# A second level of seven-product multiplication for product 6 of the gate and up stage of a two-layer encoder

## Chip, cores and metric

The kernel runs on one core of a Trainium2 chip. The metric is the device time of one execution in microseconds (us); less is better. Before the change it is 2160.32 us, the median of 3 runs (2157.54 to 2161.28).

## What is computed

Two encoder layers work on 1024 tokens of width 1024: a token mixer with memory heads, an output projection, and then a dense SwiGLU channel mixer with an inner width of 2816. The change lies in the first half of that mixer, the product `h @ w_gate_up[i]`:

```python
    for i in range(DEPTH):                                   # DEPTH = 2
        ...
        x = x + jnp.concatenate([y_tok, y_mem], axis=-1) @ w_out[i]
        h = rmsnorm(x, norm_ffn[i])
        gu = h @ w_gate_up[i]                                # (1024, 1024) @ (1024, 5632)
        x = x + (jax.nn.silu(gu[..., :D_FF]) * gu[..., D_FF:]) @ w_down[i]
    return rmsnorm(x, norm_final)
```

## The kernel before

**Precision.** Every float32 operand is kept as a rounded part and a rest (`hi`, line 105, a cast on ScalarE, ACT; `lo`, line 108, a subtraction on VectorE, DVE). A product of two operands is three matmuls (`three`, line 125): rounded by rounded, rounded by rest, rest by rounded. The weight is the operand that is loaded into the array (LDWEIGHTS, "PEld" in the profile), the activations stream past it, 512 columns at a time.

**Units and products.** The 2816 inner columns are 22 units of 128 (`Pair`, line 823). One unit holds 128 gate columns and 128 up columns; with the 1024 tokens in two halves and the 1024 rows of contraction in two halves this is a 2 by 2 by 2 block product, done in seven products instead of eight (0 to 6). Each of the seven has a contraction of 512 in four steps of 128, so it is 4 x 3 = 12 matmuls on 512 columns. The left sides are gate and up halves of the weight and their sums and differences: GpSimd (POOL) makes these in the tile `wS` (`prepare`, line 830). The right sides `B[0]` to `B[6]` are made once for each layer from the normalized activations (`right_sides`, line 965, for 1 to 6).

**Weight buffers.** `prepare` is called for every second product; it takes one tile `wgu` (tag `whl`, three buffers) that holds the left sides of two products, rounded parts and rests. Product 6 has a tile to itself. A unit so takes four tiles for its seven products. Two raw tiles for each unit are loaded by SyncE (SP) ahead of use (`load_gu`, line 926; five raw buffers).

**Sums and reads.** Products 0, 2, 4 and 6 of a unit use the PSUM bank `X`, products 1, 3 and 5 a bank `Y`. Products 2 and 4 are added in place to what `X` holds, and 5 to what 3 left in `Y`. So `read` (line 884) copies `X` after product 0 (`g1`), after 2 (`g2`) and after 4 (`c1`), and `Y` after 3 (`c2`), each copy on ACT and before the next product goes to that bank. Product 6 overwrites `X`, and DVE takes it from `c1` and multiplies by the activated gate `g1`. After every second unit `hand_over` (line 1001) writes right sides for the next stage to memory.

**Order.** `order` (lines 917 to 920) lists the products by hand: the first four units are interleaved, from the fifth on each unit runs 0 to 6. `gate_up` (line 1025) goes through it with `lead = 4`: before each product it prepares the one four places later. The recording layer puts instructions of one engine in another order than this where it expects one to be ready sooner, so the order on an engine is read from the built program. Each engine works its own list off in that order. While the last unit runs, the down projection (`left_side`, `right_side`, lines 1057 and 1100) is prepared.

Of the kernel before, what the change touches and what calls it, by code (L numbers as in the profile page):

```python
# [9 lines left out]
F32 = mybir.dt.float32  # L10
# [31 lines left out]
def trunk_kernel(ctx: ExitStack, tc: tile.TileContext, a: dict, out: bass.AP):  # L42
# [323 lines left out]
    for layer in range(2):  # L366
# [425 lines left out]


        with tc.tile_pool(name=f"fp{layer}", bufs=1, reuse_waits="tile") as fp:
            phase[:] = fp, 21, 5
            wide[:] = True, 2

            def pair(src, dst):
# [17 lines left out]
            norms = [Norm(), Norm()]  # L816

            B = [[None] * 4 for _ in range(7)]
            def load_x(m, f):
                x[m][f] = temp("x")  # L820
                nc.sync.dma_start(x[m][f], (a["x"] if is_a else x_d)[m][:, f * HS : (f + 1) * HS])

            class Pair:
# [6 lines left out]
                def prepare(self, n):  # L830

                    n -= n % 2
                    if n in self.left:
                        return
                    g1, g2 = self.raw[0][:, :HS], self.raw[0][:, HS:]
                    if n > 0:
                        u1, u2 = self.raw[1][:, :HS], self.raw[1][:, HS:]
                    sub = lambda o, p_, q_: nc.gpsimd.tensor_tensor(o, p_, q_, op=ALU.subtract)  # L838
                    s = self.raw[0]
                    if n == 2:  # L840
                        self.s = fp.tile([P, D], F32, tag="S", name="wS", bufs=2)
# [42 lines left out]
                def read(self, n):  # L884
                    self.seen.add(n)
                    X, Y = self.X, getattr(self, "Y", None)
                    add = lambda o, p_, q_, op=ALU.add: nc.vector.tensor_tensor(o, p_, q_, op=op)
                    if n == 0:
                        self.g1 = temp("g1")
                        nc.scalar.copy(self.g1, X)  # L890
                    elif n == 1:
                        add(self.g1, Y, self.g1)
                        nc.scalar.activation(self.g1, self.g1, AF.Silu)
                    elif n == 2:
                        self.g2 = temp("g2")
                        nc.scalar.copy(self.g2, X)
                    elif n == 3:
                        self.c2 = temp("c2")
                        nc.scalar.copy(self.c2, Y)  # L899
                    elif n == 4:  # L900
                        self.c1 = temp("c1")
                        nc.scalar.copy(self.c1, X)
                        add(self.c2, self.c2, self.c1)
                        if 5 in self.seen:
                            add(self.c2, self.c2, self.g2, ALU.mult)
                    elif n == 5:
                        add(self.g2, Y, self.g2)
                        nc.scalar.activation(self.g2, self.g2, AF.Silu)
                        if 4 in self.seen:
                            add(self.c2, self.c2, self.g2, ALU.mult)  # L910
                    else:
                        add(self.c1, self.c1, X, ALU.subtract)
                        add(self.c1, self.c1, self.g1, ALU.mult)

            us = [Pair(j) for j in range(NF)]
# [49 lines left out]
            def right_sides():  # L965
# [28 lines left out]
                for k in range(4):  # L994
                    B[6][k] = pair(x[k + 4][0], h_op(k))
                    yield

            def keep(i, p, t):
                nc.sync.dma_start(b_d[layer][i][:, p * HS : (p + 1) * HS], t)

# [24 lines left out]
            def gate_up():  # L1025
                run_some(rest, 1)
                load_gu()
                for i, (u, n) in enumerate(order):
                    if i + lead < len(order):
                        v, n_ = order[i + lead]  # L1030
                        v.prepare(n_)
                    u.product(n)
                    u.read(n)
                    run_some(rest, 1 if i < 2 * first else 2)
                    if n == 6 and u.j % 2:
                        hand_over(u.j // 2, us[u.j - 1], u)
                    yield u, n


            wd = a["w_dn"][layer].rearrange("(p i) r c -> p i r c", i=2)  # L1040
# [73 lines left out]
            def residual(i):  # L1114

                if i in (0, 2, 3, 4):
                    m0, f = {0: (0, 1), 2: (0, 0), 3: (4, 0), 4: (4, 1)}[i]
                    for m in range(m0, m0 + 4, 2):
                        t = fp.tile([P, 2, HS], F32, tag="S", name="xr", bufs=2)
# [83 lines left out]
            for u, n in gate_up():  # L1203
                if u.j == NF - 1 and n in (2, 3, 4):
                    keep_rows(n - 2)
                    if n > 2:
                        left_side(0, n - 3)
                if u.j == NF - 1 and n in (3, 4, 5):
                    right_side(0, n - 3)
# [127 lines left out]
```

## Time and profile before

| | |
|---|---|
| profiled execution, its own time | 2156.92 us |
| its span in the trace | 2155.1 us |
| mean granted TensorE clock | 0.993 |
| gate and up, busy of DVE / ACT / POOL in 1590 to 1670 us | 42.91 / 29.20 / 23.88 of 80 us |
| HBM read and written | 210.40 MB and 68.94 MB, 130 GB/s over the span |
| `b_d` stores of the stage | 154, of 256 KB |
| `wgu_raw` loads of the stage | 92 issues |

The rows of the profile name a line of the kernel, an engine, an operation and the tiles (out, arrow, in). In grouped rows the last number before the bar is the mean time of one instruction in ns, and after the bar stands the idle time of the engine before these instructions and who ended it. In rows of the timeline the first number is the start in us from the begin of the span, the second the length, "x12" the number of instructions merged, and the brackets hold the idle time before it and who ended that. A matmul's end is modelled, so matmuls overlap in the rows; their pace is read from starts.

### The profile page before, as it was taken

The page shows a single profiled execution, that of the slowest core. Times are in us where ns is not written, and L with a number is a line of the kernel's source. Part 1 is how long each engine was busy: PE and PEld are TensorE (multiplying, and loading weights), DVE is VectorE, ACT ScalarE, POOL GpSimd, SP SyncE. Part 2 cuts the span into 40 slices and gives each one's busy share as a digit, 9 for nine tenths or more (in the row PEclk, how much of TensorE's full clock was granted, in tenths as well). Part 3 has the DMA queues.
Part 4 walks back from the last instruction along what each step waited for, and adds up shares of the span by engine and source line. Part 5 has one row for each costly group of instructions (what it writes and reads, how often), then busy time and mean ns, then how long its engine had stood idle before and what let it go on. Part 6 is the DMA issues. An engine that isn't in the chain of part 4 may idle for free.

```text
span 2155.1 us, 28039 instructions
## 1 busy us (share of the span) xinstructions
PE 2113.1 (98%) x9946; PEld 1740.9 (81%) x9946; DVE 1417.9 (66%) x2314; ACT 1045.6 (49%) x1988; POOL 498.2 (23%) x545
## 2 busy tenths in 40 slices
PE   7999999999999999999999999999999999999997
PEld 6788888788888888888778888887888888888886
DVE  7677787776555555867776666677855564568675
ACT  6577785443333334344466566653533333344442
POOL 0344330223232320000233223203223323210000
PEclk9999999999999999999999999999999999999998
DMA  6321018323223236856232222274233222277662
GB/s 247 101 94 49 31 60 299 111 90 131 88 93 113 98 119 223 315 204 210 90 101 65 71 65 81 70 263 148 74 103 117 98 100 101 98 237 262 203 217 92
DMA packets 120076, 287.22 MB, mean 133 GB/s; under 512 B 12288, under 2 KB 18688, under 8 KB 119936
## 3 DMA queue, kind: packets, MB, share of 16 engines
q1 hardware_dynamic: 112896, 272.57, 37.8%
q10 hardware_dynamic: 7040, 12.85, 1.6%
q8 instruction: 79, 1.29, 0.2%
q14 instruction: 61, 0.50, 0.1%
HBM read 210.40 MB, written 68.94 MB: 130 GB/s over the span
## 4 chain that ended last, share of the span: by engine, by line
PE 43%; issue 4%; DVE 2%; ACT 2%; POOL 1%; DMA 0%; DVEq 0%; SPq 0%; POOLq 0%; ACTq 0%
PE X L879 11%; PE mm L139 9%; PE Y L879 8%; PE X L1171 5%; PE Y L1171 4%; PE po L139 2%; PE S L559 2%; PE O L622 1%; PE pT L602 1%; ACT p L574 0%; DMA b_raw<-b_d 0%; PE bc L242 0%; DVE pl L109 0%; DVE wqk L109 0%; PE vtr L419 0%
## 5 line engine op out<-in xcount | busy, mean ns | idle before, releaser
L879 PE MATMUL X<-hT,wgu 128*128 128x512 f32 x1056 | 259.1, 395 | 0.0
L879 PE MATMUL Y<-hB,wgu 128*128 128x512 f32 x1056 | 256.8, 392 | 1.6 <-ACT c L899 1.6
L879 PE MATMUL X<-hB,wgu 128*128 128x512 f32 x1056 | 247.8, 390 | 0.0
L1171 PE MATMUL X<-hB,wd 128*128 128x512 f32 x1056 | 242.1, 390 | 0.0
L879 PEld LDWEIGHTS X<-hT,wgu 128*128 128x128 f32 x1056 | 198.2, 188 | 47.3
L879 PEld LDWEIGHTS Y<-hB,wgu 128*128 128x128 f32 x1056 | 198.5, 188 | 46.3 <-ACT c L899 2.5
L879 PEld LDWEIGHTS X<-hB,wgu 128*128 128x128 f32 x1056 | 198.3, 188 | 41.7
L1171 PEld LDWEIGHTS X<-hB,wd 128*128 128x128 f32 x1056 | 198.1, 188 | 41.9 <-issue 1.0
L106 ACT CAST wgu<-wS 128x1024 fp32r<-128x1024 f32 x88 | 92.4, 1051 | 259.9 <-POOL wS L838 157.0
L587 POOL TENSOR_SCALAR p<-p,stat 128x384 f32<-128x384 f32 (+1 forms) x256 | 141.0, 569 | 312.1 <-DVE stat L584 212.2
L109 DVE TENSOR_TENSOR wgu<-wgu_raw,wgu 128x1024 fp32r<-128x1024 f32 (+1 forms) x88 | 84.7, 963 | 189.8 <-ACT wgu L106 189.8
L139 PE MATMUL mm<-hT,wqk 128*128 128x512 f32 x672 | 199.8, 405 | 0.1
L139 PE MATMUL po<-yT,wo 128*128 128x512 f32 x768 | 184.7, 394 | 0.0
L1171 PE MATMUL Y<-hB,wd 128*128 128x512 f32 x792 | 180.2, 389 | 0.0
L1171 PEld LDWEIGHTS Y<-hB,wd 128*128 128x128 f32 x792 | 148.7, 188 | 30.8
L139 PEld LDWEIGHTS po<-yT,wo 128*128 128x128 f32 x768 | 142.5, 188 | 29.5 <-issue 1.0
L838 POOL TENSOR_TENSOR wS<-wgu_raw 128x512 f32<-128x512 f32 x44 | 73.5, 1671 | 378.6 <-DVE wgu L109 378.6
L109 DVE TENSOR_TENSOR wgu<-wS,wgu 128x1024 fp32r<-128x1024 f32 x88 | 109.7, 1247 | 62.6 <-ACT wgu L106 62.6
L233 POOL TENSOR_TENSOR nr<-nv,neg_half 128x4 f32<-128x4 f32 (+1 forms) x11 | 11.7, 1063 | 587.0 <-DVE nv L232 586.8
L106 ACT CAST hB<-b_raw 128x512 fp32r<-128x512 f32 x154 | 88.8, 618 | 116.0 <-DMA b_raw<-b_d 106.4
L574 ACT ACTIVATE p<-p,stat 128x256 f32<-128x256 f32 (+1 forms) x192 | 112.3, 586 | 52.0 <-DVE stat L570 49.5
L106 ACT CAST wgu<-wgu_raw 128x1024 fp32r<-128x1024 f32 (+1 forms) x88 | 73.4, 835 | 122.5 <-PE Y L879 73.7
(161 smaller groups left out, 3913.3 us busy)
## 6 DMA issues: line engine op xcount, KB each, us to landing
wgu_raw<-in_w_gu SPq DMA_DIRECT2D x92, 512.0 KB
wd_raw<-in_w_dn SPq DMA_DIRECT2D x70, 512.0 KB
b_raw<-b_d SPq DMA_DIRECT2D x70, 512.0 KB
b_d<-c SPq DMA_DIRECT2D x88, 256.0 KB
b_d<-t SPq DMA_DIRECT2D x66, 256.0 KB
wo_raw<-in_w_out SPq DMA_DIRECT2D x32, 512.0 KB
x<-in_x SPq DMA_DIRECT2D x32, 256.0 KB
xr_d<-x ACTq DMA_DIRECT2D x32, 256.0 KB
```

The costliest lines, as they stand in the source:

```text
L106: nc.scalar.copy(dst, src)
L109: (eng or nc.vector).tensor_tensor(dst, src, h.bitcast(F32), op=ALU.subtract)
L139: nc.tensor.matmul(ps[:, :n], l, r, start=start and i == 0 and j == 0, stop=stop and i == len(order) - 1 and j == 2,)
L233: nc.gpsimd.tensor_tensor(r[:, :nb], v[:, :nb], neg_half[:, :nb], op=ALU.pow)
L559: nc.tensor.matmul(s_[:, :n], Q[self.h][:, qb * P : (qb + 1) * P], k, start=j == 0, stop=j == 1)
L574: nc.scalar.activation(p[:, :n], p[:, :n], AF.Exp, bias=m1, scale=-1.0, accum_out=s1)
L587: nc.gpsimd.tensor_scalar(p[:, :n], p[:, :n], ri[:, i : i + 1], 1.0, op0=ALU.mult, op1=ALU.mult)
L602: nc.tensor.transpose(tr[:, j * P : (j + 1) * P], p[:, j * P : (j + 1) * P], ident)
L622: nc.tensor.matmul(o[:, c0 : c0 + w * P], self.value(j), t[:, s0 : s0 + w].rearrange("p j q -> p (j q)"), start=j == js[0] and t is self.p ...
L838: sub = lambda o, p_, q_: nc.gpsimd.tensor_tensor(o, p_, q_, op=ALU.subtract)
L879: nc.tensor.matmul(ps, l, r, start=n in (0, 1, 3, 6) and k == 0 and i == 0, stop=k == 3 and i == 2, skip_group_check=True,)
L1171: nc.tensor.matmul(bank, l, r, start=i in (0, 1, 3, 6) and p == 0 and n == 0, stop=p == HF - 1 and n == 2, skip_group_check=True,)
```

## The change

From the fifth unit on two units a and b are taken together. Their products 6 have one right side, `B[6]`, so together they are a block product of 256 rows by a contraction of 512 by 512 columns. It is split in two in each direction and made by seven products (class `Fourth`), each of 128 rows by a contraction of 256 (two steps) by 256 columns: 7 x 2 x 3 = 42 matmuls on 256 columns, in place of 2 x 12 = 24 on 512. There are nine such pairs in each of the two layers.

- **Left sides.** `Fourth.prepare` casts the raw `u2` halves of both units into one tile `wgu` (called w4 below: a11, a12, a21, a22) and four combinations, which POOL makes with five 128x256 operations in a tile `wS4`, into another `wgu` tile (called ws4: s1 to s4). A pair takes 3 + 3 + 2 = 8 tiles, as before, from the same three buffers.
- **Right sides.** Four combinations of the blocks of `B[6]` are made once for each layer at the end of `right_sides` (eight 128x256 subtractions, four casts and four rests of 128x512; tiles `q4` and `q4h`).
- **Order.** Unit a runs 0 to 5, unit b runs 0, 1, 2, 4, then piece A, product 3 of b, piece B, product 5 of b, piece C. A is a11 and a12 (12 matmuls), B is s2 and s1 (12), C is s3, s4 and a22 (18). A, B and C use one bank of `Y`'s pool and the bank `O`.
- **Reads.** DVE subtracts the pieces from `c1` of a and b. Since b runs 4 before 3, the sum of `c2` and `c1` moves to whichever comes later.
- The pools change to 26 buffers for 128x512 tiles (from 21) and three for `wS` (from two); the kernel asks for 1024 bytes of scratch for DMA descriptors. At the end of the stage the down projection's first loads are hung on the new order's last places.

```diff
-            phase[:] = fp, 21, 5
+            phase[:] = fp, 26, 5
...
                     elif n == 3:
                         self.c2 = temp("c2")
                         nc.scalar.copy(self.c2, Y)
+                        if 4 in self.seen:
+                            add(self.c2, self.c2, self.c1)
                     elif n == 4:
                         self.c1 = temp("c1")
                         nc.scalar.copy(self.c1, X)
-                        add(self.c2, self.c2, self.c1)
+                        if 3 in self.seen:
+                            add(self.c2, self.c2, self.c1)
...
+            class Fourth:
+                def prepare(self, n):
+                    if self.w is not None:
+                        return
+                    r, h = [u.raw[1][:, HS:] for u in self.units], HS // 2
+                    s = fp.tile([P, D], F32, tag="S", name="wS4", bufs=3)
+                    s1, s2, s3, s4 = (s[:, i * h : (i + 1) * h] for i in range(4))
+                    sub = lambda o, p_, q_: nc.gpsimd.tensor_tensor(o, p_, q_, op=ALU.subtract)
+                    nc.gpsimd.tensor_tensor(s1, r[1][:, :h], r[1][:, h:], op=ALU.add)
+                    sub(s3, r[0][:, :h], r[1][:, :h])
+                    sub(s2, s1, r[0][:, :h])
+                    sub(s4, r[0][:, h:], s2)
+                    w = wp.tile([P, 2, D], F32R, tag="whl", name="wgu", bufs=3)
+                    for i in range(2):
+                        c = slice(i * HS, (i + 1) * HS)
+                        hi(w[:, 0, c], r[i])
+                        lo(w[:, 1, c], r[i], w[:, 0, c])
+                    ws = wp.tile([P, 2, D], F32R, tag="whl", name="wgu", bufs=3)
+                    hi(ws[:, 0], s)
+                    lo(ws[:, 1], s, ws[:, 0])
...
+                    load_gu()
+                    load_gu()
+                def part(self, bank, at, left, right, start=False, stop=False):
+                    for k in range(2):
+                        kw = (left[:, 0, k * P : (k + 1) * P], left[:, 1, k * P : (k + 1) * P])
+                        for i, (l, r) in enumerate(three(kw, right(k))):
+                            nc.tensor.matmul(
+                                bank[:, at : at + HS // 2], l, r, start=start and k == 0 and i == 0,
...
+                    if n == "A":
+                        self.X = ps_t.tile([P, HS], F32, tag="T", name="X4")
+                        self.Y = ps_o.tile([P, HS], F32, tag="O", name="Y4")
+                        self.part(self.X, 0, a11, of(0, 0), start=True)
+                        self.part(self.Y, 0, a12, of(2, 0), start=True)
+                    elif n == "B":
+                        self.part(self.X, 0, s2, t2)
+                        self.part(self.Y, h, s1, t1)
+                    else:
+                        self.part(self.X, 0, s3, t3)
+                        self.part(self.Y, h, s4, of(2, h), stop=True)
+                        self.part(self.X, h, a22, t4, stop=True)
...
-            order += [(u, n) for u in us[first:] for n in range(7)]
+            for a_, b_ in zip(us[first::2], us[first + 1 :: 2]):
+                z = Fourth(a_, b_)
+                order += [(a_, n) for n in range(6)] + [(b_, n) for n in (0, 1, 2, 4)]
+                order += [(z, "A"), (b_, 3), (z, "B"), (b_, 5), (z, "C")]
```

Two places in the built program matter below. The first is the list of ACT in the second pair of the first layer, around the end of unit b. Here `wgu_5569` is w4, `wgu_5574` is ws4, `wgu_5656` the first tile of the next unit; numbers tell tiles apart, and the brackets name the engine or DMA queue whose count an instruction waits for. Before, a unit at that place reads:

```order
L890 COPY g1_5535<-X_5522 128x512 [waits DMAHW2_49,PE_49]
L106 CAST wgu_5552<-wgu_raw_5258 128x512 [waits DMAHW1_49,PE_49,Activation_49]
L893 ACTIVATE g1_5535<-g1_5535 128x512 [waits DVE_49]
L896 COPY g2_5569<-X_5522 128x512 [waits DMAHW0_49,PE_49]
L106 CAST wgu_5571<-wgu_raw_5293 128x1024 [waits DMAHW2_49,PE_49,Activation_49]
L899 COPY c2_5587<-Y_5574 128x512 [waits DMAHW3_49]
```

Now unit b of the pair reads:

```order
L897 COPY g2_5623<-X_5581 128x512 [waits DMAHW5_49,PE_49]
L905 COPY c1_5637<-X_5581 128x512 [waits DMAHW6_49,PE_49]
L106 CAST wgu_5574<-wS4_5564 128x1024 [waits PE_49,Activation_49]
L900 COPY c2_5672<-Y_5659 128x512
L106 CAST wgu_5656<-wgu_raw_5284 128x1024 [waits DMAHW2_49,PE_49,Activation_49]
```

Before, the cast for product 6 (`wgu_5552`) stands right behind the read of product 0, four products ahead of its use. Now the cast of ws4 stands behind the reads of products 2 and 4 of b, and the copy of `Y` behind it, which reads product 3, has no wait for PE of its own: the cast's wait already covers the end of product 3. In the built program the count that the cast waits for is that of the last matmul of product 3 of b, in all 18 pairs: ws4 gets the buffer of the tile that holds products 2 and 3 of b.

The second place is the list of PE behind it, from the last matmuls of product 3 of b (`Y_5659<-hT8_4571`) into piece B and product 5 (`wgu_5544`):

```order
L880 MATMUL Y_5659<-hT8_4571,wgu_5524 128x512 x6
L954 MATMUL X4_5639<-q4h_4910,wgu_5574 128x256 [waits DVE_49,Activation_49]
L954 MATMUL X4_5639<-q4h_4911,wgu_5574 128x256
L954 MATMUL Y4_5640<-q4h_4884,wgu_5574 128x256 [waits DVE_49]
L954 MATMUL Y4_5640<-q4h_4885,wgu_5574 128x256
L880 MATMUL Y_5659<-hB_4702,wgu_5544 128x512 [waits Activation_49]
L880 MATMUL Y_5659<-hB_4702,wgu_5544 128x512 x2
L880 MATMUL Y_5659<-hB_4727,wgu_5544 128x512
L954 MATMUL X4_5639<-q4h_4910,wgu_5574 128x256 [waits DVE_49]
```

Before, the list of PE goes on behind product 3 with product 4 on the other bank:

```order
L879 MATMUL Y_5574<-hT8_4571,wgu_5483 128x512 x6
L879 MATMUL X_5522<-hT8_4759,wgu_5517 128x512 [waits Activation_49]
L879 MATMUL X_5522<-hT8_4759,wgu_5517 128x512
L879 MATMUL X_5522<-hT8_4759,wgu_5517 128x512 [waits DVE_49]
L879 MATMUL X_5522<-hT8_4759,wgu_5517 128x512 x3
```

So the first matmul behind product 3 of b now reads ws4. Where product 4 of unit b starts, the list of PE now reads:

```order
L880 MATMUL X_5581<-hT8_4663,wgu_5524 128x512 x6
L954 MATMUL X4_5639<-hB_4800,wgu_5569 128x256 [waits Activation_49]
L954 MATMUL X4_5639<-hB_4800,wgu_5569 128x256
L954 MATMUL X4_5639<-hB_4800,wgu_5569 128x256 [waits DVE_49]
L954 MATMUL X4_5639<-hB_4822,wgu_5569 128x256 x3
L880 MATMUL X_5581<-hT8_4759,wgu_5544 128x512 [waits Activation_49]
```

Half of piece A (six matmuls) has been put ahead of product 4, which waits for ACT's copy of `X` after product 2. Before, product 3 stood there.

More of the change, by code (lines that the diff above doesn't have):

```diff
@@ L818, in trunk_kernel @@
             B = [[None] * 4 for _ in range(7)]
+            fourth = []
             def load_x(m, f):
@@ L840, in prepare @@
                     if n == 2:
-                        self.s = fp.tile([P, D], F32, tag="S", name="wS", bufs=2)
+                        self.s = fp.tile([P, D], F32, tag="S", name="wS", bufs=3)
                     if n in (2, 4):
@@ L996, in right_sides @@
                     yield
+                h = HS // 2
+                blocks = [(x[k + 4][0][:, :h], x[k + 4][0][:, h:]) for k in range(4)]
+                t = [temp("q4").rearrange("p (k c) -> p k c", k=2) for _ in range(4)]
+                for k in range(2):
+                    (b11, b12), (b21, b22) = blocks[k], blocks[k + 2]
+                    sub(t[0][:, k], b12, b11)
+                    sub(t[1][:, k], b22, t[0][:, k])
+                    sub(t[2][:, k], b22, b12)
+                    sub(t[3][:, k], t[1][:, k], b21)
+                    yield
+                for s in t:
+                    f = [fp.tile([P, 2, h], F32R, tag="t2k", name="q4h", bufs=26) for _ in range(2)]
+                    hi(f[0], s)
+                    lo(f[1], s, f[0])
+                    fourth.append(f)
+                    yield
             def keep(i, p, t):
@@ L1036, in gate_up @@
                         hand_over(u.j // 2, us[u.j - 1], u)
-                    yield u, n
+                    if n == "C":
+                        hand_over(u.units[0].j // 2, *u.units)
+                    yield i - len(order)
             wd = a["w_dn"][layer].rearrange("(p i) r c -> p i r c", i=2)
@@ L1118, in residual @@
                     for m in range(m0, m0 + 4, 2):
-                        t = fp.tile([P, 2, HS], F32, tag="S", name="xr", bufs=2)
+                        t = fp.tile([P, 2, HS], F32, tag="S", name="xr", bufs=3)
                         nc.sync.dma_start(
@@ L1201, in finish @@
                     nc.scalar.dma_start(out[:2].rearrange("k p t -> p k t")[:, :, at:], first)
[L1203 to L1209, printed above, removed]
+            for to_go in gate_up():
+                if -6 <= to_go <= -4:
+                    keep_rows(to_go + 6)
+                    if to_go > -6:
+                        left_side(0, to_go + 5)
+                if -5 <= to_go <= -3:
+                    right_side(0, to_go + 5)
             norms = [Norm(), Norm() if is_a else Norm(HS, 7)]
@@ L1324 @@
     from concourse.bass_utils import run_bass_kernel_spmd
-    nc = bacc.Bacc("TRN2", target_bir_lowering=False, num_devices=1)
+    nc = bacc.Bacc("TRN2", target_bir_lowering=False, num_devices=1, dynamic_dma_scratch_size=1024)
     arrays, args = {}, {}
```

30 lines of the change are left out of this document (added).

## Prediction

> **What bounds the kernel now.** First the page's busy table and slices:
>
> ```profile
> span 2155.1 us, 28039 instructions
> PE 2113.1 (98%) x9946; PEld 1740.9 (81%) x9946; DVE 1417.9 (66%) x2314; ACT 1045.6 (49%) x1988; POOL 498.2 (23%) x545
> PE   7999999999999999999999999999999999999997
> DVE  7677787776555555867776666677855564568675
> PEclk9999999999999999999999999999999999999998
> ```
>
> PE has work in every slice at full clock. Next the waits of PE in 500 to 900 us, which hold the paired units of the first layer:
>
> ```profile
> engine line waited for: us in total, times, longest us
> PE Y L879 <- ACT c L899: 0.8, 1, 0.8
> ```
>
> One wait of 0.8 us in 400. So the stage is bound by the pace of matmuls, and any new wait of PE is paid in full. The pace, and what it costs to wait, is read from the timeline of one unit:
>
> ```profile
> 699.88 1.23 DVE L109 TENSOR_TENSOR wgu<-wS,wgu 128x1024 fp32r<-128x1024 f32 x1 [0.45 <-ACT wgu L106]
> 701.18 1.68 POOL L838 TENSOR_TENSOR wS<-wgu_raw 128x512 f32<-128x512 f32 x1 [8.63 <-DVE wgu L109]
> 702.82 1.74 POOL L838 TENSOR_TENSOR wS<-wgu_raw,wS 128x512 f32<-128x512 f32 x1
> 703.76 2.68 PEld L879 LDWEIGHTS Y<-hB,wgu 128*128 128x128 f32 x12
> 703.98 2.88 PE L879 MATMUL Y<-hB,wgu 128*128 128x512 f32 x12
> 704.59 1.05 ACT L106 CAST wgu<-wS 128x1024 fp32r<-128x1024 f32 x1 [4.21 <-POOL wS L838]
> ...
> 709.49 2.96 PE L879 MATMUL Y<-hT,wgu 128*128 128x512 f32 x12
> 709.69 0.59 ACT L896 COPY g<-X 128x512 f32<-128x512 f32 x1 [1.38 <-PE X L879]
> 712.29 2.96 PE L879 MATMUL X<-hT,wgu 128*128 128x512 f32 x12
> 712.54 1.05 ACT L106 CAST wgu<-wgu_raw 128x1024 fp32r<-128x1024 f32 x1 [2.26 <-PE Y L879]
> 713.49 0.58 ACT L899 COPY c<-Y 128x512 f32<-128x512 f32 x1
> 713.62 1.22 DVE L109 TENSOR_TENSOR wgu<-wgu_raw,wgu 128x1024 fp32r<-128x1024 f32 x1 [5.33 <-ACT wgu L106]
> ...
> 717.83 5.60 PE L879 MATMUL X<-hB,wgu 128*128 128x512 f32 x24
> 723.27 2.88 PE L879 MATMUL Y<-hB,wgu 128*128 128x512 f32 x12
> ```
>
> 24 matmuls take 723.27 - 717.83 = 5.44 us, 0.227 each. A cast that waits for the end of a product starts 0.25 after the next product's first matmul (712.54 against 712.29), a copy out of PSUM 0.20 after (709.69 against 709.49). A cast lasts 1.05; the copy behind it starts 0.95 after its start. A weight load runs 0.22 ahead of its matmul (703.76 against 703.98).
>
> **What is removed and added on PE.** A pair loses 24 matmuls on 512 columns, 24 x 0.227 = 5.45 us, and gains 42 on 256. The gate stage has none of those; the memory projection at the start has, each with its own weight, here its weight loads in an unbroken stretch:
>
> ```profile
> 17.18 4.23 PEld L139 LDWEIGHTS mm<-mhl,wm 128*128 128x128 f32 x35
> ```
>
> Without the last load's own 0.19 that is 4.04 over 34 steps, 0.119 each and not half of 0.227. 42 x 0.119 = 5.00, so a pair saves **0.45 us**, 18 pairs 8.1. At best it is 0.1135, half a wide one (saves 0.68 a pair), at worst, with all 4.23 over 33, 0.128 (saves 0.07). I take the nearest row. The Trainium skill, "TensorE: Matmul & The Clock Gate", section "Back-to-back issue gap", gives N / 2.4 + 2.5 ns for an isolated matmul, 109 and 216 ns here, and by it a pair would save 0.6; both rows are slower than that, the narrow one by more, and the measurement decides.
>
> **The wait before piece B.** The list of ACT shows the cast of ws4 waiting for the end of b's product 3, and the next matmul of PE reads ws4. Nothing can cover it: all work of PE behind stands in line. From the moment at which the next matmul would have started: 0.25 until the cast starts, 1.05 for the cast, then the wake-up of PE, which another stall shows:
>
> ```profile
> 44.63 1.21 DVE L109 TENSOR_TENSOR wf<-wf_raw,wf 128x1024 fp32r<-128x1024 f32 x1
> 45.89 2.17 PEld L139 LDWEIGHTS mm<-hT,wf 128*128 128x128 f32 x10 [1.65 <-DVE wf L109]
> 45.90 2.37 PE L139 MATMUL mm<-hT,wf 128*128 128x512 f32 x9 [1.45 <-DVE wf L109]
> ```
>
> The subtraction ends at 45.84 and the load starts 0.05 later; that the load can't run ahead costs its 0.22. Sum 0.25 + 1.05 + 0.05 + 0.22 = **1.57 us** a pair, 28.3 in 18. Without the 0.22 it is 1.35 (24 us), and if the copy of `Y` behind the cast (0.58) came in full on top, 2.15 (39). I take 1.57, because the copy starts 0.95 after the cast and so ends at 0.25 + 0.95 + 0.58 = 1.78 after that moment, while four matmuls of B run from 1.57 to 2.04, and product 5's first weight load is due at 1.82. The rests of ws4 (DVE, 1.22 from 0.03 after the cast) are ready at 2.55; product 5's four matmuls fill PE to 2.95.
>
> **Four smaller waits,** each worked out from the same rows.
> - Product 4 of b waits for the copy of `X` after product 2: 0.20 + 0.59 + 0.05 + 0.22 = 1.06, behind six narrow matmuls (6 x 0.119 = 0.71) where twelve wide ones stood. Left over 0.34, 18 times: 6.1 us.
> - Product 4 of a, in 16 of 18 pairs: there the list of PE runs product 3 ahead of 2, and only four wide matmuls (0.91) stand between 2 and 4. Left over 0.15: 2.4.
> - The next pair's first tile takes the buffer that b's product 5 frees. Cast and rests end 0.25 + 1.05 + 0.03 + 1.22 = 2.55 after that; with 0.27 to the matmul, 2.82. Piece C and two wide matmuls cover 18 x 0.119 + 0.45 = 2.59. Left over 0.23, 18 times: 4.1.
> - Product 2 of a waits for the copy of `X` after 0. On ACT that copy now stands behind a cast that waits for POOL. From the end of b's product 5: rests of the first tile until 2.55, a product on DVE, rests of the second from 3.1 to 4.3, then as in the rows from 699.88 on POOL to 7.8 (1.68 + 1.74), two casts 0.95 apart, the copy until 10.3, with 0.27 to the matmul 10.5. PE by then has C, two products and eleven matmuls, 2.14 + 0.23 + 35 x 0.227 = 10.3. Left over 0.2, 16 times: 3.2.
>
> Together 15.8, from nothing, if the recorded order has slack that I don't see, to twice as much.
>
> **What costs nothing.** The new right sides: eight subtractions and four rests on DVE, from this row 0.42 for a 128x256 one, and 0.69 for a 128x512:
>
> ```profile
> L219 DVE TENSOR_TENSOR sq<-sq 128x256 f32<-128x256 f32 x7 | 2.5, 420 | 0.0
> 450.57 0.69 DVE L887 TENSOR_TENSOR g<-Y,g 128x512 f32<-128x512 f32 x1 [0.60 <-PE Y L879]
> 454.01 0.69 DVE L109 TENSOR_TENSOR wgu<-wgu_raw,wgu 128x512 fp32r<-128x512 f32 x1 [2.75 <-ACT wgu L106]
> 457.32 1.23 DVE L109 TENSOR_TENSOR wgu<-wS,wgu 128x1024 fp32r<-128x1024 f32 x1 [1.29 <-ACT wgu L106]
> ```
>
> That is 8 x 0.42 + 4 x 0.69 = 6.1 us beside 4.6 of idle at this place, with PE's need some 2 us later; without that cover 1.5 for each layer. POOL's five operations for `wS4` (at half a 1.68 each, 4.2 us a pair) are issued nearly a pair ahead. DVE's reads of A, B and C are on other banks than the next product's. Loads by SP are issued about a pair before use, and the number is the same.
>
> **The sum.** 28.3 + 15.8 - 8.1 = +36.0 us. On the profiled execution's own time, 2156.92 (span 2155.1 and 1.8 around it), that is 2192.9. The median before is 3.4 above that execution; on it, 2160.3 + 36.0 = **2196.3**.
>
> **Rivals.**
> - Only the wait at piece B is new, the small ones have cover: +28.3 - 8.1 = 20.2, so 2180.5. For it: idle of ACT and DVE in this stage. Against: the sums above stand on the list's order.
> - Not slower: the cast of ws4 isn't held, as with the cast for product 6 before, which ran four products early; the saving alone would stand, 2152. It decides at a wait of 0.45 us a pair. Against it: the list of ACT, and one buffer too few for anything else.
> - The clock falls. A pair gets a stop of about 1.4 us; elsewhere stops come with clocks like these (in the rows of windows the third number from the end):
>
> ```profile
> 25.49 0.50 PE L139 MATMUL mm<-mhl,wm 128*128 128x256 f32 x2 [3.19 <-ACT wm L106]
> 91.37 1.60 PE L602 MATMUL pT<-ident,p 128*128 128x128 f32 x6 [1.81 <-POOL p L587]
> 25.00:30.00 5.00, 3.72 (x16) 3.21 (x17) 4.50 (x7) 1.91 (x4) 0.00 (x0) 0.72 1.05 395
> 44.00:56.00 12.00, 8.81 (x43) 6.23 (x43) 11.91 (x23) 7.35 (x16) 0.02 (x1) 1.00 0.23 74
> 88.00:100.00 12.00, 10.17 (x51) 7.89 (x50) 5.37 (x15) 7.58 (x25) 9.24 (x16) 0.86 0.05 16
> ```
>
>   (Ahead of it stand the busy times of PE, PEld, DVE, ACT and POOL, behind it the DMA share and GB/s.) After 3.19 the clock is 0.72, around 1.81 it is 0.86, around 1.45 it is 1.00. If each stop cost what 88 to 100 shows, 0.14 of 12 us = 1.7, 18 stops give 30: 2226. The stop here is nearest to the row that kept 1.00. The Trainium skill, same page, section "A second HAM failure mode: psum-queue depth-cycling", has short idles between groups of matmuls bring the clock down again and again; the row from 44 to 56 speaks against it at this length.
> - POOL becomes the pace: its 4.2 us more a pair fall into the chain of the fourth small wait, 16 x 4.2 = 67, so 2263. Against: those operations come ahead of the pair's chain, and POOL is idle 8.63 us before the row at 701.18.
>
> **Chances.** Forecast 0.57, only the main wait 0.25, clock 0.08, POOL 0.04, not slower 0.06. The range takes in the forecast and the main wait alone: from 20.2 less 4 for its short form (2176) to 36.0 with the small waits a bit over double or the long form of the main one (2216). Within 0.2% (4.3 us, about what a measurement here can tell from no change) would need a wait of about half a microsecond a pair: 0.02; faster by more 0.04, slower by more 0.94.
>
> **What would show it.** In the profile after: PE idle before piece B's first matmul, ended by the cast of ws4, of about 1.2 to 1.4 us in all 18 pairs; 0.119 from one narrow matmul to the next; some 324 more matmuls; the clock unchanged. Wrong would be: no idle there, or most of the added time on other lines than B's and products 2 and 4.

## The result and the profile after

| | before | after |
|---|---|---|
| median of the runs | 2160.41 us (5 runs, 2157.54 to 2161.28) | 2194.53 us (5 runs, 2191.73 to 2199.08) |
| span of the profiled execution | 2155.1 us | 2190.0 us |
| mean granted clock | 0.993 | 0.993 |

The ratio is 1.017, with a 95% interval from 1.0159 to 1.0181: 34 us slower. The page of the changed kernel, its busy table and slices:

```profile
span 2190.0 us, 28996 instructions
PE 2121.5 (97%) x10270; PEld 1749.2 (80%) x10270; DVE 1493.2 (68%) x2464; ACT 1063.2 (49%) x2014; POOL 557.4 (25%) x617
PE   7999999999999999999999999999999999999997
PEclk9999999999999999999999999999999999999998
```

PE has 324 matmuls more (10270 against 9946), as 18 pairs x 18 make; the clock is as before. The slices hide what happened: a wait of 1.2 us in every 40 is 3%, which no digit shows. The waits of PE in 500 to 930 us, nine pairs and a third of the down stage of the first layer, show it:

```profile
PE X L954 <- ACT wgu L106: 10.8, 9, 1.3
PE Y L1276 <- DVE x L1244: 0.4, 1, 0.4
```

Nine waits for a cast, one in each pair, where the view of before has one wait of 0.8 us. The timeline of one pair around piece B:

```profile
561.50 2.94 PE L880 MATMUL Y<-hT,wgu 128*128 128x512 f32 x12
...
564.53 1.04 ACT L106 CAST wgu<-wS 128x1024 fp32r<-128x1024 f32 x1 [2.96 <-PE Y L880]
565.48 0.58 ACT L900 COPY c<-Y 128x512 f32<-128x512 f32 x1
565.61 1.23 DVE L109 TENSOR_TENSOR wgu<-wS,wgu 128x1024 fp32r<-128x1024 f32 x1 [3.03 <-ACT wgu L106]
565.63 0.30 PEld L954 LDWEIGHTS X<-q4h,wgu 128*128 128x128 f32 x2 [1.62 <-ACT wgu L106]
565.63 0.50 PE L954 MATMUL X<-q4h,wgu 128*128 128x256 f32 x2 [1.19 <-ACT wgu L106]
...
565.97 0.40 PE L954 MATMUL Y<-q4h,wgu 128*128 128x256 f32 x2
...
566.20 1.11 PE L880 MATMUL Y<-hB,wgu 128*128 128x512 f32 x4
...
569.72 0.39 PE L880 MATMUL Y<-hB,wgu 128*128 128x512 f32 x1
569.94 0.88 PE L954 MATMUL X<-q4h,wgu 128*128 128x256 f32 x6
...
570.66 0.88 PE L954 MATMUL Y<-hB,wgu 128*128 128x256 f32 x6
```

Product 3 of b fills PE from 561.50. The cast of ws4 has waited since 561.57 (2.96 before 564.53) for its end, and PE waits for the cast. The last matmul of product 3 starts at 564.04 in the trace, so the next was due at 564.27; it comes at 565.63, **1.36 us** late: 0.26 to the start of the cast, 1.04 for the cast, 0.06 to the load. At the second matmul of B another 0.10 is lost (the third starts at 565.97, and 565.97 - 565.63 = 0.34 holds two narrow ones and this loss). Six narrow matmuls take 570.66 - 569.94 = 0.72, 0.12 each.

Counted in the same way over the starts of all PE matmuls (what a start comes later than 0.227 us behind a wide one, 0.119 behind a narrow one), the 34.9 us between the two spans are these:

| where | us |
|---|---|
| before piece B, 18 pairs (1.46 in most) | +27.1 |
| small waits at products 2 and 4 and the next pair's first tile | +9.9 |
| matmuls: saved | -7.4 |
| start of the gate stage, PE waits for the sums of squares | +2.9 |
| two single waits of about 1 us of the stage of before that are gone | -1.9 |
| down stage, two layers | +3.3 |
| ahead of the first gate stage | +1.0 |

The last row is no effect of the change: the code there is the same, and in the kernels below that stretch ends anywhere between 407.3 and 411.8 us. For the saving, the pairs of the last experiment below repeat every 38.30 us, with 0.14 of small waits in each, against 38.57 before: 38.57 - 38.16 = 0.41 a pair.

### The profile page after: what moved, and what is told of

Same layout as the page of the kernel before. It is cut to its first block, busy times and chain, and to the rows that moved or that the text cites. A ratio compares the mean times of both kernels' runs of the same rounds, so it can differ in the third digit from the quotient of the medians.

```text
span 2190.0 us, 28996 instructions
## 1 busy us (share of the span) xinstructions
PE 2121.5 (97%) x10270; PEld 1749.2 (80%) x10270; DVE 1493.2 (68%) x2464; ACT 1063.2 (49%) x2014; POOL 557.4 (25%) x617
## 3 DMA queue, kind: packets, MB, share of 16 engines
q8 instruction: 81, 1.33, 0.2%
## 4 chain that ended last, share of the span: by engine, by line
PE 75%; issue 13%; DVE 5%; ACT 4%; DMA 2%; POOL 1%; SPq 0%; DVEq 0%; ACTq 0%; POOLq 0%
PE X L880 16%; PE Y L880 15%; PE mm L139 13%; PE po L139 8%; PE X L1276 5%; PE Y L1276 3%; PE S L559 3%; PE O L622 3%; PE pT L602 3%; PE X L954 2%; PE Y L954 2%; ACT wgu L106 1%; DVE wgu L109 1%; DMA wm_raw<-in_w_mem 1%; DMA b_raw<-b_d 1%
## 5 line engine op out<-in xcount | busy, mean ns | idle before, releaser
L106 ACT CAST wgu<-wS 128x1024 fp32r<-128x1024 f32 x106 | 111.1, 1048 | 200.2 <-POOL wS L839 91.5
L109 DVE TENSOR_TENSOR wgu<-wS,wgu 128x1024 fp32r<-128x1024 f32 x106 | 130.5, 1231 | 94.4 <-ACT wgu L106 94.4
L1276 PEld LDWEIGHTS Y<-hB,wd 128*128 128x128 f32 x792 | 148.4, 188 | 34.1 <-ACT wd L106 1.9
L880 PE MATMUL X<-hB,wgu 128*128 128x512 f32 x624 | 156.6, 396 | 0.1
L846 POOL TENSOR_TENSOR wS<-wgu_raw 128x512 f32<-128x512 f32 x44 | 59.5, 1352 | 357.3 <-DMA wgu_raw<-in_w_gu 340.3
L880 PEld LDWEIGHTS X<-hB,wgu 128*128 128x128 f32 x624 | 114.9, 188 | 30.7 <-DVE wgu L109 7.9
L109 DVE TENSOR_TENSOR pl<-pT,ph 128x384 fp32r<-128x384 f32 (+1 forms) x256 | 118.7, 494 | 20.7 <-ACT ph L106 17.7
L880 PE MATMUL Y<-hT,wgu 128*128 128x512 f32 x528 | 131.8, 395 | 0.0
```

What stands on the lines that cost most here:

```text
L106: nc.scalar.copy(dst, src)
L109: (eng or nc.vector).tensor_tensor(dst, src, h.bitcast(F32), op=ALU.subtract)
L880: nc.tensor.matmul(ps, l, r, start=n in (0, 1, 3, 6) and k == 0 and i == 0, stop=k == 3 and i == 2, skip_group_check=True,)
L1276: nc.tensor.matmul(bank, l, r, start=i in (0, 1, 3, 6) and p == 0 and n == 0, stop=p == HF - 1 and n == 2, skip_group_check=True,)
```

## Experiments

Theory: ws4 has the buffer of the tile with b's products 2 and 3, so its cast starts only when product 3 ends, and PE stands for it. Rivals: the stop costs time for another reason than the cast; or the second level costs its time wherever it stands.

**1. A shorter cast.**

```diff
-                    hi(ws[:, 0], s)
-                    lo(ws[:, 1], s, ws[:, 0])
+                    for i in (1, 0, 2, 3):
+                        c = slice(i * h, (i + 1) * h)
+                        hi(ws[:, 0, c], s[:, c])
+                        lo(ws[:, 1, c], s[:, c], ws[:, 0, c])
```

> The changed kernel (2194.5 us), with the cast of ws4 and its rests made in four pieces of 128x256, s2 first, so that the first matmul of piece B needs a quarter of the cast. Theory one, the added time is PE standing still while ws4 is cast (1.05 of the 1.46 us lost per pair before B): a quarter piece, by halving from 0.59 for 512 columns, lasts some 0.35, so the loss falls by 0.7 to about 0.8 us a pair, 18 x 0.7 = 12 us in all: 2180 to 2186 us. Rival, the loss hangs on the stop as such (a restart of PE, its queue, the clock), whatever the cast lasts: no more than 3 us less, 2191 to 2195.

Measured: 2186.1 us, ratio to the kernel before 1.013 (1.011 to 1.0149), so 8.4 us less than the change. Its waits in 500 to 930 us:

```profile
PE X L956 <- ACT wgu L106: 5.8, 9, 1.5
```

One pair in its timeline:

```profile
602.63 1.33 ACT L106 CAST wgu<-wS 128x256 fp32r<-128x256 f32 x4 [2.96 <-PE Y L880]
603.07 1.43 DVE L109 TENSOR_TENSOR wgu<-wS,wgu 128x256 fp32r<-128x256 f32 x4 [2.39 <-ACT wgu L106]
603.09 0.30 PEld L956 LDWEIGHTS X<-q4h,wgu 128*128 128x128 f32 x2 [0.98 <-ACT wgu L106]
603.09 0.50 PE L956 MATMUL X<-q4h,wgu 128*128 128x256 f32 x2 [0.55 <-ACT wgu L106]
```

PE starts 0.46 us after the first cast began, where it was 1.10, and the idle falls from 1.19 to 0.55. So the length of the wait is the length of the cast. By the starts of the matmuls the wait itself is 11.1 us shorter in the 18 pairs, near the 12 expected. Two things take some of it back: the fourth matmul of B now starts 0.07 late (1.3 us in all), behind a weight load at 603.39 that comes 0.05 after the end of the second cast, and the waits for DVE in the down stage are 1.5 us longer. The 0.10 at the second matmul is as in the change.

**2. A buffer of its own.**

```diff
-                    ws = wp.tile([P, 2, D], F32R, tag="whl", name="wgu", bufs=3)
+                    ws = fp.tile([P, 2, D], F32R, tag="ws4", name="wgu4", bufs=1)
...
-            phase[:] = fp, 26, 5
+            phase[:] = fp, 22, 5
...
```

> The changed kernel, with ws4 in a buffer of its own (the pool of 128x512 tiles falls from 26 to 22 to make room), so that its cast need not wait for the end of b's product 3. Theory one, the buffer is the cause of the wait before B: that wait goes in all 18 pairs, 18 x 1.46 = 26 us, and the small waits in other places (about 10 us in all) stay, since their order is the same: 2166 to 2171 us, still above the kernel before. Rival one, the time comes from the narrow matmuls or the order of b's products, and the wait at B only collects it: below 8 us less, 2186 or above. Rival two, the four buffers less hold up other tiles: the wait goes but as much comes back on lines of product 0 to 5.

Measured: 2182.7 us, ratio 1.0109 (1.0092 to 1.0126), above the 2166 to 2171 expected. The waits of PE in 480 to 840 us:

```profile
PE X L880 <- ACT g L897: 3.8, 5, 0.9
PE X L880 <- ACT c L905: 3.3, 1, 3.3
```

The windows around the longest of them (the third number from the end is the granted clock):

```profile
485.00:489.00 4.00, 0.83 (x4) 0.34 (x2) 0.90 (x1) 1.98 (x4) 1.91 (x3) 1.00 0.00 0
489.00:493.00 4.00, 3.88 (x10) 3.06 (x11) 3.96 (x6) 1.51 (x3) 0.00 (x0) 0.57 0.49 141
```

The wait before B is gone from the list: the buffer is its cause. But of its 27 us only 12 come back. The cast of ws4, which now needs no PE, stands earlier in ACT's list, and in the first pair of each layer it waits there for POOL, whose sums wait for a load; the copy of `X` that PE needs (`c`, L905) is behind it. PE stands 3.3 us, and the clock is 0.57 in the 4 us after. In both layers together six later pairs lose about 1 us at product 4 of a. So rival two was the nearer one, although it is the order on ACT that holds things up, and no want of small buffers that the trace shows.

**3. Product 3 earlier.** The pieces move instead, so that product 3 of b ends long before ws4 is needed.

```diff
-                order += [(a_, n) for n in range(6)] + [(b_, n) for n in (0, 1, 2, 4)]
-                order += [(z, "A"), (b_, 3), (z, "B"), (b_, 5), (z, "C")]
+                order += [(a_, n) for n in range(6)] + [(b_, n) for n in range(5)]
+                order += [(z, "A"), (b_, 5), (z, "B"), (z, "C")]
```

> The changed kernel, with another order of unit b: 0 to 4, then A, 5, B, C. Product 3 then ends 12 wide matmuls (product 4) and piece A and product 5 before B, and product 4 has product 3 ahead of it as before the change. Theory one, the added time is the wait at B (26 us) and the wait of b's product 4 (0.24 us x 18 = 4.6): both go, which gives 2164, and the pieces B and C on one bank may add up to 0.2 us a pair: 2162 to 2168; with the saving of 8 us alone left it would be 2152. Rival, the second level costs its time wherever it stands (narrow matmuls, extra work on DVE and POOL): 2185 or more.

Measured: 2173.0 us, ratio 1.0059 (1.0047 to 1.0072), 5 us above the range expected: the wait at B and that of b's product 4 are gone, and a new one is there. Its waits in 500 to 840 us:

```profile
PE X L880 <- ACT g L897: 4.7, 8, 1.5
```

The timeline at the border of two pairs:

```profile
618.44 1.29 POOL L846 TENSOR_TENSOR wS<-wgu_raw 128x512 f32<-128x512 f32 x1 [4.00 <-DMA wgu_raw<-in_w_gu]
618.50 2.31 DVE L109 TENSOR_TENSOR wgu<-wgu_raw,wgu 128x1024 fp32r<-128x1024 f32 x1
...
619.80 2.14 POOL L839 TENSOR_TENSOR wS<-wS,wgu_raw 128x512 f32<-128x512 f32 x1
...
620.74 0.68 DVE L888 TENSOR_TENSOR g<-Y,g 128x512 f32<-128x512 f32 x1
621.45 0.63 ACT L894 ACTIVATE g<-g 128x512 f32<-128x512 f32 x1 [4.41 <-DVE g L888]
621.98 0.57 ACT L897 COPY g<-X 128x512 f32<-128x512 f32 x1
...
622.60 3.06 PE L880 MATMUL X<-hT,wgu 128*128 128x512 f32 x12 [1.54 <-ACT g L897]
```

Read backwards: product 4 of a waits for the copy of `X`, which stands on ACT behind the activation, which has waited 4.41 us for DVE, whose subtraction of rests lasts 2.31 us beside a POOL operation where it takes 1.23 alone. In the change the same copy is in time, or late by 0.4 us at most; that the 1.4 us before each piece B gave it this room is my reading, and experiments 9 to 11 go after the chain itself.

**4. The order alone.** The kernel before, with every second unit from the fifth on in the order 0, 1, 2, 4, 3, 5, 6 (the sum of `c2` and `c1` moves as in the change).

```diff
-            order += [(u, n) for u in us[first:] for n in range(7)]
+            for a_, b_ in zip(us[first::2], us[first + 1 :: 2]):
+                order += [(a_, n) for n in range(7)] + [(b_, n) for n in (0, 1, 2, 4, 3, 5, 6)]
```

> The kernel before (2160.4 us), with only the order of every second unit changed to 0, 1, 2, 4, 3, 5, 6: no second level. Product 4 then stands right behind 2 on the same bank, and waits for the copy of X: 0.20 + 0.59 + 0.05 and about 0.1 for the load that can't run ahead, 0.94 us, 18 times. Theory one, what I put the small wait of product 4 down to: 2160 + 17 = 2174 to 2180. Rival, the program's list puts other matmuls in between, as it does with half of piece A in the change: 2159 to 2163, and the wait is not one of the order of the products alone.

Measured: 2192.8 us, ratio 1.015 (1.0136 to 1.0164). Neither expectation held. Its longest group of waits in 500 to 930 us:

```profile
PE X L879 <- ACT g L890: 11.9, 8, 1.5
```

The end of one pair and the begin of the next in its timeline:

```profile
566.31 1.98 PE L879 MATMUL X<-hB,wgu 128*128 128x512 f32 x8
...
568.14 3.06 PE L879 MATMUL Y<-hB,wgu 128*128 128x512 f32 x12
...
571.03 3.79 PE L879 MATMUL X<-hB,wgu 128*128 128x512 f32 x16
...
571.29 1.05 ACT L106 CAST wgu<-wS 128x1024 fp32r<-128x1024 f32 x1 [3.20 <-PE Y L879]
```

Product 4 has no wait of note, since the program's list puts matmuls of product 3 in between. But product 2 of the next unit waits 1.5 us at all eight borders between the pairs. Product 5 now stands right behind 3 on the same bank and needs the copy of `Y`; the list bridges that with 8 matmuls of product 6, which before stood behind 5 (x24 at 717.83 in the prediction's timeline, with the next unit's product 0; x16 here). The cast at 571.29 waits for the end of product 5, and from it runs the chain of rests, POOL's sums, cast and copy to the next product 2; PE arrives there 8 x 0.227 = 1.8 us earlier than before. So the order of the products alone costs this kernel as much as the whole change did, with no second level in it.

**5 and 6. The pools.** The pools of the change alone, in the kernel before (also the third `xr` buffer and the scratch, not printed below); and the change with two buffers for `wS`, `wS4` and `xr`.

```diff
-            phase[:] = fp, 21, 5
+            phase[:] = fp, 26, 5
...
-                        self.s = fp.tile([P, D], F32, tag="S", name="wS", bufs=2)
+                        self.s = fp.tile([P, D], F32, tag="S", name="wS", bufs=3)
...
```

> The kernel before (2160.4 us), with only the pool sizes and the scratch of the change: 26 buffers for 128x512 tiles, three for wS and xr, 1024 bytes of scratch; no second level. Theory one, the third wS buffer lets POOL start its sums while DVE adds the squares at the start of the gate stage, and both then run slower (the additions 1.78 and 1.63 us where 0.69 and 1.66 stood): PE's first wait for them grows from 1.07 to about 2.1 in layer 0 and 2.9 in layer 1, together 2.9 us: 2162 to 2165 us. Rival, that longer wait comes with the new right sides or the new order, and the pools alone change nothing: 2159 to 2161.

> The changed kernel (2194.5 us), with two buffers for wS, wS4 and xr in place of three. Theory one, the third buffer is what lengthens the wait at the start of the gate stage: it goes back to 1.07, 2.9 us less, and the wait before piece B stays at 1.46, since its cast waits for PE and not for the sums: 2190 to 2193 us. Rival, the sums of a pair need the third buffer (POOL has five operations more in each pair): a wait for POOL of some 1 to 2 us a pair, 2205 or more.

Measured: 2166.2 us for the pools alone, ratio 1.0034 (1.0022 to 1.0047), 1 us above the range expected, and 2194.2 us for the change with two buffers, ratio 1.0166 (1.0152 to 1.018), where 2190 to 2193 was expected. PE's waits at the start of the first gate stage, in this order: before, the change, the pools alone, the change with two buffers, each apart.

```profile
PE st L212 <- DVE sq L219: 0.9, 1, 0.9
```

```profile
PE st L212 <- DVE sq L219: 2.0, 1, 2.0
```

```profile
PE st L212 <- DVE sq L219: 2.1, 1, 2.1
```

```profile
PE st L212 <- DVE sq L219: 0.9, 1, 0.9
```

The wait follows the buffers, not the second level (in the second layer it is 0.9, 2.8, 3.1 and 0.9). What happens is in the timelines of POOL and DVE of the changed kernel there:

```profile
410.21 2.23 POOL L839 TENSOR_TENSOR wS<-wS,wgu_raw 128x512 f32<-128x512 f32 x1
412.40 1.71 POOL L839 TENSOR_TENSOR wS<-wgu_raw 128x512 f32<-128x512 f32 x1
...
411.20 1.78 DVE L219 TENSOR_TENSOR sq<-sq 128x512 f32<-128x512 f32 x1
...
413.02 1.63 DVE L219 TENSOR_TENSOR sq<-sq 128x512 f32<-128x512 f32 x1
```

An addition that takes 0.69 alone takes 1.78 and 1.63, ending about 0.55 behind the POOL operation beside it (412.98 against 412.44, 414.65 against 414.11): DVE stands while POOL reads, then works. With two buffers one of the two additions runs undisturbed, because POOL still waits for a buffer. The Trainium skill, "SBUF — State Buffer", section "SBUF: two separate sides", has a lock for this: the two engines share a pair of ports, and whichever starts first holds it for its whole instruction. These rows agree. With two buffers the start was 2.9 us shorter as expected, but at the next pair's first tile about 0.35 us was lost where it had been 0.11, the down stage was 1.5 us longer, and the total is the same.

**7 and 8. Two buffers in the natural order; later loads.** Experiment 3 with the buffers of 6; and this with the down projection's first loads one place later.

```diff
-                if -6 <= to_go <= -4:
-                    keep_rows(to_go + 6)
+                if -5 <= to_go <= -3:
+                    keep_rows(to_go + 5)
...
```

> The order 0 to 4, A, 5, B, C for unit b (2173.0 us as measured), with two buffers for wS, wS4 and xr in place of three. In that kernel product 4 of a waits 0.6 to 1.7 us in 16 pairs (10.8 us in all) for a copy that stands on ACT behind the activated gate, which waits for DVE, whose subtraction of rests lasts 2.31 us beside a POOL operation in place of 1.23. Theory one, with two buffers POOL runs at another time and both this wait and the one at the start of the stage (2.9 us) shrink: 2160 to 2166. Rival, POOL's sums come too late with two buffers and are waited for in their place: 2175 or more.

> As the kernel with the order 0 to 4, A, 5, B, C and two buffers for wS, wS4 and xr, with the first loads of the down projection hung one place later, at the places counted from the end that they had before the change. Theory one, the waits of 1 to 2 us in the down stage of the changed kernel (3.1 us in the two layers beyond those of before) come from the place of these loads in SP's queue: 1 to 3 us less than that kernel. Rival, they come from the stores and loads of the last pair, whose order differs: no difference beyond 0.5 us, or more, since the loads come later.

Measured: 2195.0 us, ratio 1.0172 (1.0158 to 1.0186), and 2196.2 us, ratio 1.018 (1.0166 to 1.0194). Theory one fell in both: the waits for the same copy grow, here in 500 to 840 us of the first of the two, and the later place of the loads gains nothing.

```profile
PE X L880 <- ACT g L897: 16.8, 8, 2.1
```

With two buffers POOL makes its sums for `wS4` just beside DVE's work at the border, and DVE's subtractions of 0.69 there become 1.23. Behind four of these 16 waits the clock falls too, and the pair then takes 42.2 us in place of 40.6.

**9, 10 and 11. The chain at the border.** All three have the order of experiment 3. In the first a22 moves from C to A, so that w4 comes free earlier; the second also records `hand_over` after the next pair's product 2; the third has two buffers besides.

```diff
                         self.part(self.Y, 0, a12, of(2, 0), start=True)
+                        self.part(self.X, h, a22, t4)
...
-                        self.part(self.X, h, a22, t4, stop=True)
...
                     if n == "C":
-                        hand_over(u.units[0].j // 2, *u.units)
+                        held.append((u.units[0].j // 2, *u.units))
+                    if held and (n == 2 or i == len(order) - 1):
+                        hand_over(*held.pop())
...
```

> The order 0 to 4, A, 5, B, C for unit b (2173.0 us as measured, 10.8 us of it a wait of a's product 4, which stands behind a chain over the pair's border: the cast of the next tile waits for the end of piece C, which frees w4, then DVE, POOL, the cast of the sums, the copies). Here a22, the last piece that reads w4, is moved from C to A, so that w4 is free some 4 us earlier. Theory one, the buffer of w4 sets that chain: the wait of a's product 4 goes or falls below 0.2 us a pair, 2160 to 2165 us. Rival, DVE's own list at the border (four subtractions for the next stage ahead of the rests and of the gate) sets it: no more than 4 us less, 2169 to 2173.

> As the kernel with a22 in A, and besides the four subtractions for the next stage are recorded after the next pair's product 2 and not right behind piece C, so that DVE makes the gate sum and the rests first; product 3 of a then stands whole behind product 2. Theory one, the two together leave no wait of a at the border: 2157 to 2163 us, about the time of the kernel before, because the longer wait at the start of the stage (2.9 us), the down stage (3 us) and 2 us ahead of the stage eat the 8 us saved. Rival, product 2 of a, with nothing of product 3 ahead of it, waits 0.9 us for the copy of X after 0 (as it stood in the trace of the order 0 to 4, A, 5, B, C: it was due at 615.3, the copy would end at 616.1): 2170 or more.

> As the kernel before it in this set, with two buffers for wS, wS4 and xr in place of three. Theory one, the wait at the start of the stage goes back to 1.07 us in both layers and the border, now freed earlier, bears two buffers: 2.9 us less than that kernel, 2154 to 2160 us, which could be below the kernel before. Rival, two buffers make POOL's sums late at the border as they did with the natural order (2195.0): 2170 or more.

Measured, beside a kernel before at 2158.35 us: 2170.5 us (1.0053, 1.004 to 1.0067), 2162.4 us (1.0021, 1.0012 to 1.0029) and **2155.5 us (0.9984, 0.9975 to 0.9993)**. The waits of PE in 500 to 930 us, of the first, and of the third:

```profile
PE X L880 <- ACT g L897: 3.4, 7, 1.3
PE Y L954 <- DVE c L980: 0.9, 1, 0.9
```

```profile
PE Y L954 <- DVE c L980: 1.1, 1, 1.1
```

Freeing the buffer alone gave 2.5 us, the rival's case, and the two intervals do not tell that from nothing (the wait falls from 10.8 to 9.1 us in the profiles). With DVE's list shortened as well, a further 8.1 us, the wait is gone; DVE's list alone was not run. The third is the only version here below the kernel before. It is 6.8 us faster than the second where 2.9 was expected: the 2.9 at the start of the stage is there. The second also has waits at product 2 in the first pair of each layer (1.7 us with what follows) and one of 1.0 at the last pair of the first layer, which the third has not; why is open.

The gate stages gain more than the total shows. The profiled executions of the third kernel and of the kernel before have the same span, 2155.1 us; the two gate stages are 6.8 us shorter in it, the down stages 4.4 longer, and the stretch ahead of the first gate stage, whose code is the same, 2.6 longer.

## Why the prediction was right, and where its sizes were off

Predicted were +36.0 us, measured +34.1 in the medians; the range held it. By its own steps:

- **The wait before B** was the step that carried it, and it stands: idle of 1.19 us in 15 of 18 pairs and 1.33 to 1.53 in the others, ended by the cast of ws4. Experiment 1 shows that its length is the cast's, experiment 2 that the buffer causes it. 27.1 us against 28.3. Of the four numbers 0.25, 1.05 and 0.05 came out as 0.26, 1.04 and 0.06; the 0.22 for the load that can't run ahead was too much, 0.10 was lost.
- **The small waits** came to 9.9 us, not 15.8. Product 4 of b lost 0.24 a pair where I had 0.34, and the next pair's first tile 0.11 where I had 0.23, in both the same 0.1 too much for the load. Product 2 of a, put at 0.20, waits in no pair but the first of each layer (0.7): from the end of b's product 5 (569.95) the copy ends at 579.55, after 9.6 us, where my chain had 10.3; PE comes to product 2 at 580.22, the 10.3 that I had for it. POOL's two sums made the difference: they end 7.1 after that moment (1.29 and 1.48 us long), where I took 7.8 (1.68 and 1.74).

```profile
578.97 0.58 ACT L891 COPY g<-X 128x512 f32<-128x512 f32 x1
...
580.22 2.96 PE L880 MATMUL X<-hT,wgu 128*128 128x512 f32 x12
```

- **The saving** was 0.41 us a pair instead of 0.45, from the narrow pace of 0.12 as read from the memory projection.
- **"What costs nothing" was wrong in one thing.** I looked at the new right sides and at POOL's operations in the pairs, and not at the third `wS` buffer, which lets POOL run on beside DVE at the begin of the stage. That costs 2.9 us, shown by experiments 5 and 6. The right sides themselves show no wait. I also counted POOL's operations for `wS4` wrongly, here and in the rival on POOL: the program has four in each pair, not five (617 - 545 = 72 on POOL in 18 pairs), of 0.73 to 1.11 us.
- **The down stage** is 3.3 us longer, which I had at nothing. The longest wait that I followed there is for DVE's read of a bank, behind its work on loads that land late:

```profile
2011.35 1.23 DVE L1185 TENSOR_TENSOR wd_kept<-wd_raw 128x1024 f32<-128x1024 f32 x1 [1.72 <-DMA wd_raw<-in_w_dn]
...
2019.91 3.31 PE L1276 MATMUL Y<-hB,wd 128*128 128x512 f32 x12 [1.49 <-DVE x L1244]
```

  The pools alone lengthen this stage by 2.4 us, and with two `xr` buffers it stays long. But experiment 4, with the pools of before and no second level, has it 3.1 us longer as well, so the pools are not needed for it. The cause is open.
- **The rivals.** "Only the main wait" (2180.5) is out by the small waits and the two misses. The clock stayed at 1.00 in the pairs: 500 to 850 us and 1610 to 1960 us have a mean of 1.00, and so do the windows below, behind the stop shown above. The rule on short idles between groups of matmuls, weighed in the prediction from the Trainium skill ("TensorE: Matmul & The Clock Gate", section "A second HAM failure mode: psum-queue depth-cycling"), does not show here, with idles of 1.2 us.

```profile
565.00:569.00 4.00, 3.37 (x20) 3.05 (x21) 2.67 (x4) 1.06 (x2) 2.09 (x3) 1.00 0.00 0
569.00:573.00 4.00, 4.00 (x27) 3.49 (x26) 2.42 (x3) 2.52 (x3) 1.16 (x2) 1.00 0.00 0
```

So the total was nearer than its parts, and that is luck: 5.9 us too much for the small waits and 6.2 too little for two places that I passed over (2.9 and 3.3) nearly cancel.

## What to carry to other kernels

When a product is moved later in a hand-written order, look up who gets its buffer next, and whether that one's first step stands ahead of PE's next matmul: here the wait that this made cost 27 us, against a saving of 7. A wait that is taken away shows the next chain, which it had hidden: the first repair gave back 12 us, the second 22, and only with the border of the pairs rearranged as well did the second level pay, by 0.16% (0.07% to 0.25%). A buffer more is not free if it lets one engine run beside another that it slows.

## What the runs showed of the hardware

- DVE and POOL slow each other by whole instructions: 128x512 additions of 0.69 us took 1.63 and 1.78 beside POOL, the 128x1024 subtraction of 1.23 took 2.31, and POOL's sums of 1.3 took 2.1 to 2.2.
- The length of one stop of PE does not settle whether the clock falls. Behind the 18 stops of 1.2 to 1.5 us of the changed kernel it stayed at 1.00. Experiment 7 has 16 stops of 2.08 to 2.13 us: behind 12 of them it stayed at 1.00, behind four it was 0.57 to 0.74 in the next 4 us. After 2.8 us at the start of the second gate stage of the changed kernel it was 0.63 for the next 4 us, and after 3.3 us (experiment 2) 0.57. In the kernel before, 0.59 stands there in 1501 to 1505 us behind a stop of 0.9 us. I had taken 0.86 around a stop of 1.81 us for a sign of what such stops do, but that window held much else.

```profile
1519.00:1523.00 4.00, 4.00 (x16) 2.81 (x16) 0.86 (x2) 0.00 (x0) 1.02 (x1) 0.63 0.43 131
```

```profile
622.00:626.00 4.00, 3.58 (x16) 2.94 (x17) 1.23 (x1) 2.29 (x4) 0.86 (x1) 1.00 0.01 2
744.00:748.00 4.00, 3.67 (x9) 2.94 (x10) 1.23 (x1) 1.71 (x3) 0.96 (x1) 0.57 0.01 4
```

(The first row is of the changed kernel, the other two are of experiment 7, each right behind one of its stops.)
